# Inverting the 16x16 diagonal blocks of a gated DeltaNet once per group on 128 partitions

## The chip, the cores and the metric

One core of one Trainium2 chip runs the whole program in one launch. The metric is the device time in microseconds (us) from start to end; lower is better. The kernel before is given by three runs, and by one profiled execution from which all rows below come.

## What is computed

Two layers of a model: layer 0 is a bidirectional chunked gated DeltaNet, layer 1 a differential attention. Both work on 512 tokens (256 context, 256 latent) of width 2048. The change touches layer 0 alone, and in it the inverse `tinv` of a unit lower triangular matrix per chunk, head and direction:

```python
lower = jnp.where(strict, jnp.einsum('nbhid,nbhjd->nbhij', kb, kc) * decay, 0.0)
tinv = lax.linalg.triangular_solve(eye + lower, eye, left_side=True, lower=True, unit_diagonal=True)
u = tinv @ (vc * bc[..., None])
w = tinv @ (kb * jnp.exp(gc)[..., None])

def step(s, inp):
    q_i, k_i, u_i, w_i, a_i, gl_i = inp
    v_new = u_i - w_i @ s
    o_i = q_i @ s + a_i @ v_new
    s = s * gl_i[..., None, None] + jnp.einsum('bhck,bhcv->bhkv', k_i, v_new)
```

There are 16 key heads with two value heads each, two directions, and the kernel uses chunks of 128 tokens, so 4 chunks: 2 directions x 4 chunks x 2 value heads = 16 matrices of 128x128 for each key head.

## The kernel before

A **group** g is one key head with its two value heads; there are 16 (g0 to g15). Its four chunks form two **halves** of two. The DeltaNet stage is written as generators (`stream_...`, `filler`), which a small driver (`Drive`) interleaves by priority, by estimated costs and by counted resources (for example `m`: 4, so that the matrices of two groups can be in work). The scheduler of the framework then orders each engine's instructions again by a timeline of its own; every engine runs its list strictly in order.

- `filler` (priority 9, the lowest) makes the projections. One projection tile is 48 matmuls of 128x512 into `pj`; a group has six: q, k, v0, v1, z0, z1. Their weights come in by DMA on SP's queue and are split into two parts by ScalarE (L205, hi) and GpSimd (L207, lo).
- `stream_m` (L741) makes, per half, the matrices I + lower: the products k k^T in `gq`, the decay `grm` (L704, L706), the scaling to `ma` (L712), GpSimd adds the identity (L762), and ScalarE casts to `m16` (L764). `m16` holds eight 128x128 matrices of one half.
- `block_inv` (L715), called once per half, inverts the 16x16 blocks on the diagonal, eight per matrix, 64 blocks in a half. The half is written to HBM (`mb_d`, L718) and its diagonal blocks are read back with one block on each of 64 partitions (`bk`, L720, in pieces of 16 numbers). Then VectorE solves row by row on 64 partitions: two operations make X, the negated block (L725, L726); then for each row i from 1 to 15 one product `bP` (L729) and one sum `bY` (L731). I call these 32 operations a **chain**; each one needs the one before. ScalarE casts the result (L734, L735), and two DMAs put it on the diagonals of two zeroed buffers in HBM (`tu_d`, L737). The tiles of a chain have one buffer each, so chains follow one another.
- `stream_lev` (L770, one for each chunk of a half) loads the block diagonal inverses as `T` and `U` (L791) and merges blocks in three levels (16 to 32, 64, 128): matmuls into `iv`, a masked product `R` on VectorE (L800), casts on ScalarE. The result is `uf`.
- `stream_b` (priority 1) carries the state through the chunks, four steps per group, with matmuls into `sb` and `so` and VectorE operations between them (`y` L891, `yb` L922, `x` L928, `S` L938, `O` L949).
- `stream_at` makes the attention within chunks; `stream_ada` works off modulation rows for later on GpSimd and ScalarE (`rp`, L150, L151).

The wait that ties `stream_m` to the levels before it stands at L748: the matrices of group g, half h, are made only when both chunks' T and U of group g-1, half h, have been loaded, since `mb_d` and `tu_d` have two copies, one per half:

```python
                if g > 0:
                    for p in range(2):
                        yield ev("ld", g - 1, half, p)
```

## Time and profile before

| | us |
|---|---|
| median of 3 runs | 3188.47 |
| fastest and slowest run | 3186.46, 3197.45 |
| span of the profiled execution, first to last instruction | 3172.3 |
| what lies around that span, up to the median run | 16.2 |

The profile gives the span of its execution and no other time of it. Engines are PE (TensorE, matmuls), PEld (its weight loads), DVE (VectorE), ACT (ScalarE), POOL (GpSimd) and SP (the queue that issues nearly all DMAs). A row of groups gives line, engine, operation, written and read tiles, shapes, count, then total busy us and mean ns of one, then the engine's idle time just before it and what ended that. PEclk is the granted share of TensorE's full clock. A busy TensorE is not TensorE at its peak, since matmuls overlap in its pipeline.

### The profile page before, as it was taken

What the parts mean: (1) busy time and instruction counts of PE and PEld (TensorE: products, weight loads), DVE (VectorE), ACT (ScalarE), POOL (GpSimd) and SP (SyncE); (2) the same over time, 40 slices, a digit from 0 to 9 for tenths busy, and PEclk for the clock granted to TensorE, in tenths of its full rate; (3) what the DMA queues carried; (4) which work ended last, traced back from release to release, by engine and by line L of the source; (5) the groups of instructions that cost most, each with busy time, mean ns of one, the idle gap of its engine ahead of it and who ended that gap; (6) DMA issues with size and microseconds to landing.
All of it is one profiled execution on the core that took longest, in us unless ns stands there. A gap on an engine that the chain in (4) does not pass through costs nothing. (4 is left out here: it accounts for less than half of the span.)

```text
span 3172.3 us, 52230 instructions
## 1 busy us (share of the span) xinstructions
PE 2850.3 (90%) x15822; PEld 2251.3 (71%) x15822; DVE 2098.0 (66%) x4728; ACT 1860.8 (59%) x5447; POOL 2052.4 (65%) x2370
## 2 busy tenths in 40 slices
PE   7777898998988898988989988899898999999998
PEld 3455676676776676766767766677686888888888
DVE  7977767769669778678678679632334654544454
ACT  4255675666766666666766756655456665534353
POOL 5876686777777677777767767466466676622334
PEclk8798999998999999999989989999999999999999
DMA  9634445445545555445445445656744555433345
GB/s 336 236 101 115 125 132 123 127 127 131 133 125 134 122 131 134 127 121 136 128 118 142 125 116 131 178 169 192 230 146 129 152 160 161 142 111 110 115 127 163
DMA packets 507185, 457.03 MB, mean 144 GB/s; under 512 B 241171, under 2 KB 383251, under 8 KB 502803
## 3 DMA queue, kind: packets, MB, share of 16 engines
q1 hardware_dynamic: 506900, 453.68, 51.5%
q8 instruction: 124, 2.03, 0.3%
q14 instruction: 159, 1.30, 0.2%
q10 hardware_dynamic: 2, 0.02, 0.0%
HBM read 427.18 MB, written 26.36 MB: 143 GB/s over the span
## 5 line engine op out<-in xcount | busy, mean ns | idle before, releaser
L151 ACT ACTIVATE rp<-rp 128x256 f32<-128x256 f32 x1024 | 426.5, 417 | 344.7 <-POOL rp L150 341.4
L729 DVE TENSOR_TENSOR bP<-bX,bY 64x1 f32<-64x1 f32 (+14 forms) x480 | 225.6, 470 | 15.0 <-ACT bY L727 6.9
L704 DVE SCALAR_TENSOR_TENSOR gra<-gra,gct,cs 128x128 f32<-128x128 f32 x256 | 108.6, 465 | 132.9 <-DMA gra<-gc_d 132.3
L151 ACT ACTIVATION_READ_ACCUMULATOR rp<-rp 128x1 f32 x1024 | 193.8, 189 | 0.0
L704 DVE SCALAR_TENSOR_TENSOR grm<-grm,gct,cs 128x128 f32<-128x128 f32 x256 | 142.7, 602 | 66.3 <-DMA grm<-gc_d 65.6
L800 DVE TENSOR_TENSOR R<-iv,lv 128x512 f16<-128x512 f32 x192 | 126.0, 679 | 29.2 <-PE iv L88 28.8
L167 DVE CUSTOM_DVE_ANT_0 aj<-ar,crow 128x1024 bf16<-128x1024 f32 x80 | 116.3, 1454 | 11.2 <-DMA ar<-in_adaw_dram 9.9
L706 ACT ACTIVATE grm<-grm 128x512 f32<-128x512 f32 x64 | 40.3, 630 | 135.3 <-DVE grm L704 135.3
L762 POOL TENSOR_TENSOR ma<-ma,cs 128x512 f32<-128x512 f32 x64 | 84.8, 1325 | 48.4 <-DVE ma L712 34.7
L731 DVE TENSOR_REDUCE bY<-bP 64x1 f32<-64x1 f32 (+14 forms) x480 | 108.7, 227 | 8.8
L88 PE MATMUL iv<-U,R 128*128 128x128 f16 x768 | 77.2, 225 | 38.3 <-DVE R L800 33.0
L88 PEld LDWEIGHTS <-m 128*128 128x128 f16 x1024 | 73.4, 100 | 51.8 <-issue 46.5
L88 PEld LDWEIGHTS <-R 128*128 128x128 f16 x768 | 47.8, 101 | 83.7 <-DVE R L800 45.7
L706 ACT ACTIVATE gra<-gra 128x512 f32<-128x512 f32 x64 | 40.4, 631 | 106.6 <-DVE gra L704 106.4
L88 PE MATMUL sb<-x,kx 128*128 128x128 f32 x384 | 59.3, 300 | 28.1 <-DVE x L928 28.1
L712 DVE SCALAR_TENSOR_TENSOR at<-gra,beta,gq 128x128 f32<-128x128 f32 x256 | 72.3, 335 | 17.8 <-PE so L88 17.6
L765 POOL TENSOR_TENSOR ml<-ma,m 128x512 bf16<-128x512 f32 x64 | 77.3, 1208 | 6.5 <-ACT m L764 3.2
L817 ACT CAST T<-iv 128x512 f16<-128x512 f32 x128 | 73.4, 574 | 10.4 <-PE iv L88 10.3
L88 PE MATMUL iv<-T,m 128*128 128x128 f16 x768 | 70.8, 223 | 9.5 <-DMA T<-tu_d 4.1
L88 PEld LDWEIGHTS sb<-x,kx 128*128 128x128 f32 x384 | 53.4, 208 | 36.0 <-DVE x L928 33.9
L88 PE MATMUL sb<-yb,uf 128*128 128x128 bf16 x512 | 54.2, 225 | 26.5 <-DVE yb L922 20.4
L88 PE MATMUL so<-x,at 128*128 128x128 f32 x512 | 77.2, 294 | 0.3 <-DVE x L928 0.3
(2763 smaller groups left out, 11506.7 us busy)
## 6 DMA issues: line engine op xcount, KB each, us to landing
aw<-in_adaw_dram SPq DMA_DIRECT2D x512, 128.0 KB, 3.0
ar<-in_adaw_dram SPq DMA_DIRECT2D x32, 1024.0 KB, 6.3
gra<-gc_d SPq DMA_DIRECT2D x128, 128.0 KB, 4.2
grm<-gc_d SPq DMA_DIRECT2D x128, 128.0 KB, 4.2
mb_d<-m SPq DMA_DIRECT2D x32, 256.0 KB, 4.3
U<-tu_d SPq DMA_DIRECT2D x128, 64.0 KB, 2.7
T<-tu_d SPq DMA_DIRECT2D x128, 64.0 KB, 2.5
yd<-sz SPq DMA_DIRECT2D x32, 256.0 KB, 2.9
```

What stands on the lines that cost most here:

```text
L88: nc.tensor.matmul(o, l, r, start=start, stop=stop)
L151: nc.scalar.activation(pr, pr, AF.Copy, accum_out=acc[:, s, q:q + 1])
L167: nc.vector.tensor_tensor_reduce(jk, rq, cr, 1.0, 0.0, ALU.mult, ALU.add, a)
L704: nc.vector.scalar_tensor_tensor(gr[:, u], gr[:, u], gct[:, c, dd, 2 * g + h:2 * g + h + 1], gam[:, s, dd], ALU.subtract, ALU.min)
L706: nc.scalar.activation(gr, gr, AF.Exp)
L712: nc.vector.scalar_tensor_tensor(o[:, u], gr[:, u], beta[:, c, dd, 2 * g + h:2 * g + h + 1], pg, ALU.mult, ALU.mult)
L729: nc.vector.tensor_tensor(pr[:, :i, :i], X[:, i, :i].unsqueeze(1).to_broadcast([64, i, i]), Y[:, :i, :i].rearrange("p j c -> p c j"), ALU. ...
L731: nc.vector.tensor_reduce(Y[:, i, :i], pr[:, :i, :i], AX.X, ALU.add)
L762: nc.gpsimd.tensor_tensor(ma, ma, ident.unsqueeze(1).to_broadcast([P, 4, P]), ALU.add)
L765: nc.gpsimd.tensor_tensor(ml[:, :, k], mv, m16[:, :, k], ALU.subtract)
L800: nc.vector.tensor_tensor(R, quad(pp), lvb(n), ALU.mult)
L817: nc.scalar.copy(Tm, quad(pt))
```

## The change

`block_inv` runs once per group, when both halves' matrices are there, on 128 partitions: 2 directions x 4 chunks x 2 heads x 8 blocks. The buffers `mb_d` and `tu_d` hold 16 matrices in place of 8, and their two copies alternate by group. Each half is written to `mb_d` in two DMAs, one per direction. Both halves' levels wait for the one inversion. `stream_m` waits for the loads of T and U of group g-2, all four chunks, before the first half. The zeroing of `tu_d` takes eight DMAs in place of four.

```diff
@@ -246,8 +246,8 @@
     yd = dram.tile([HV, P, T], F32, name="yd")
     xs_d = dram.tile([KT, P, T], F32, name="xs_d")
     sc_d = dram.tile([2, D], F32, name="sc_d")
-    mb_d = [dram.tile([8, US], F16, name=f"mb_d{i}") for i in range(2)]
-    tu_d = [[dram.tile([8, US], F16, name=f"tu_d{i}{j}") for j in range(2)] for i in range(2)]
+    mb_d = [dram.tile([16, US], F16, name=f"mb_d{i}") for i in range(2)]
+    tu_d = [[dram.tile([16, US], F16, name=f"tu_d{i}{j}") for j in range(2)] for i in range(2)]
     gc_d = dram.tile([NCH, NU, P], F32, name="gc_d")
 
     hp = pool("hp", reuse_waits="tile")
@@ -381,10 +381,11 @@
     zt = dl.tile([P, 1024], F16, name="zt", tag="m16", bufs=4)
     nc.vector.memset(zt, 0.0)
     full = lambda a: a.rearrange("u (j i) -> j u i", i=P)[:P]
-    diag = lambda a: bass.AP(tensor=a[:].tensor, offset=a[:].offset, ap=[[16 * P + 16, 64], [P, 16], [1, 16]])
+    diag = lambda a: bass.AP(tensor=a[:].tensor, offset=a[:].offset, ap=[[16 * P + 16, P], [P, 16], [1, 16]])
     for i in range(2):
         for j in range(2):
-            nc.sync.dma_start(full(tu_d[i][j]), zt.rearrange("p (u i) -> p u i", u=8))
+            for k in range(2):
+                nc.sync.dma_start(full(tu_d[i][j])[:, 8 * k:8 * k + 8], zt.rearrange("p (u i) -> p u i", u=8))
 
     convw = load_small("convw", [P, 4 * KT, 5], d["convw"], dl)
     adt = load_small("adt", [P, 2, 2, HV], d["adt"].to_broadcast([P, NB]).rearrange("p (k d h) -> p k d h", k=2, d=2), dl)
@@ -712,41 +713,40 @@
             nc.vector.scalar_tensor_tensor(o[:, u], gr[:, u], beta[:, c, dd, 2 * g + h:2 * g + h + 1], pg,
                                            ALU.mult, ALU.mult)
 
-    def block_inv(g, half, m16):
-        par = half
-        nm = f"{g}{half}"
-        nc.sync.dma_start(full(mb_d[par]), m16.rearrange("p d c h i -> p (d c h) i"))
-        bk = dl.tile([64, 16, 16], F16, tag="bk", name=f"bk{nm}", bufs=1)
+    def block_inv(g):
+        par = g % 2
+        bk = dl.tile([P, 16, 16], F16, tag="bk", name=f"bk{g}", bufs=1)
         nc.sync.dma_start(bk, diag(mb_d[par]))
-        X = dl.tile([64, 16, 16], F32, tag="bX", name=f"bX{nm}", bufs=1)
-        Y = dl.tile([64, 16, 16], F32, tag="bY", name=f"bY{nm}", bufs=1)
-        pr = dl.tile([64, 16, 16], F32, tag="bP", name=f"bP{nm}", bufs=1)
-        TU = dl.tile([64, 2, 16, 16], F16, tag="bT", name=f"bT{nm}", bufs=1)
-        nc.vector.tensor_scalar(X[:32], bk[:32].rearrange("p j i -> p i j"), -1.0, None, ALU.mult)
-        nc.vector.tensor_scalar(X[32:], bk[32:], -1.0, None, ALU.mult)
-        nc.scalar.copy(Y, e16[:64])
+        X = dl.tile([P, 16, 16], F32, tag="bX", name=f"bX{g}", bufs=1)
+        Y = dl.tile([P, 16, 16], F32, tag="bY", name=f"bY{g}", bufs=1)
+        pr = dl.tile([P, 16, 16], F32, tag="bP", name=f"bP{g}", bufs=1)
+        TU = dl.tile([P, 2, 16, 16], F16, tag="bT", name=f"bT{g}", bufs=1)
+        nc.vector.tensor_scalar(X[:64], bk[:64].rearrange("p j i -> p i j"), -1.0, None, ALU.mult)
+        nc.vector.tensor_scalar(X[64:], bk[64:], -1.0, None, ALU.mult)
+        nc.scalar.copy(Y, e16)
         for i in range(1, 16):
-            nc.vector.tensor_tensor(pr[:, :i, :i], X[:, i, :i].unsqueeze(1).to_broadcast([64, i, i]),
+            nc.vector.tensor_tensor(pr[:, :i, :i], X[:, i, :i].unsqueeze(1).to_broadcast([P, i, i]),
                                     Y[:, :i, :i].rearrange("p j c -> p c j"), ALU.mult)
             nc.vector.tensor_reduce(Y[:, i, :i], pr[:, :i, :i], AX.X, ALU.add)
         for dd in range(2):
-            ps_ = slice(32 * dd, 32 * dd + 32)
+            ps_ = slice(64 * dd, 64 * dd + 64)
             nc.scalar.copy(TU[ps_, dd], Y[ps_])
             nc.scalar.copy(TU[ps_, 1 - dd], Y[ps_].rearrange("p j i -> p i j"))
         for j in range(2):
             nc.sync.dma_start(diag(tu_d[par][j]), TU[:, j])
-        return [tu_d[par][j].rearrange("(d c h) (j i) -> c j d h i", d=2, c=2, i=P) for j in range(2)]
+        return [tu_d[par][j].rearrange("(d c h) (j i) -> c j d h i", d=2, c=4, i=P) for j in range(2)]
 
     def stream_m():
         for g in range(G):
             yield ev("kT", g)
             kT = sts[g]["kT"]
+            if g > 1:
+                for half in range(2):
+                    for p in range(2):
+                        yield ev("ld", g - 2, half, p)
             for half in range(2):
                 yield ("m", 1)
                 yield ("gq", 1)
-                if g > 0:
-                    for p in range(2):
-                        yield ev("ld", g - 1, half, p)
                 nm = f"{g}{half}"
                 m16 = dl.tile([P, 2, 2, 2, P], F16, tag="m16", name=f"m16{nm}", bufs=4)
                 ml = dl.tile([P, 2, 2, 2, P], BF16, tag="ml", name=f"ml{nm}", bufs=4)
@@ -764,8 +764,13 @@
                     nc.scalar.copy(m16[:, :, k], mv)
                     nc.gpsimd.tensor_tensor(ml[:, :, k], mv, m16[:, :, k], ALU.subtract)
                 sts[g].setdefault("m", []).append((m16, ml))
-                sts[g].setdefault("tu", []).append(block_inv(g, half, m16))
-                dr.set("tu", g, half, lat=32)
+                for dd in range(2):
+                    u = 8 * dd + 4 * half
+                    nc.sync.dma_start(full(mb_d[g % 2])[:, u:u + 4], m16[:, dd].rearrange("p c h i -> p (c h) i"))
+                if half == 1:
+                    sts[g]["tu"] = block_inv(g)
+                    for hf in range(2):
+                        dr.set("tu", g, hf, lat=32)
                 free("gq", 1, 14)
                 yield 0.44, 12.0 * LX
 
@@ -779,7 +784,7 @@
                 st = sts[g]
                 c = 2 * half + p
                 m16 = st["m"][half][0]
-                tu = st["tu"][half]
+                tu = st["tu"]
 
                 def t16(tag):
                     return dl.tile([P, 4, P], F16, tag=f"{tag}{p}", name=f"{tag}{g}{c}", bufs=1)
@@ -788,7 +793,7 @@
                 Tm, U = t16("T"), t16("U")
                 for dst, src in ((Tm, tu[0]), (U, tu[1])):
                     for dd in range(2):
-                        nc.sync.dma_start(dst[:, 2 * dd:2 * dd + 2], src[p, :P, dd])
+                        nc.sync.dma_start(dst[:, 2 * dd:2 * dd + 2], src[c, :P, dd])
                 dr.set("ld", g, half, p)
                 yield 0.0, 4.0
                 for n in range(4, 7):

```

The number of chains falls from 32 to 16, and VectorE's list changes where they stand. Inside the first chain of group 4 the list of VectorE had this in the middle (tiles: `grm` decay, `at` attention within the chunk, `S` state, `sz` gate):

```order
L729 TENSOR_TENSOR bP_6891<-bX_6889,bY_6890 64x6x6
L704 SCALAR_TENSOR_TENSOR grm_8098<-grm_8098,gct,cs 128x128 x2
L731 TENSOR_REDUCE bY_6890<-bP_6891 64x6
L704 SCALAR_TENSOR_TENSOR grm_8098<-grm_8098,gct,cs 128x128 x2
L729 TENSOR_TENSOR bP_6891<-bX_6889,bY_6890 64x7x7
L712 SCALAR_TENSOR_TENSOR at_7486<-gra_7478,beta,gq 128x128 x4
L731 TENSOR_REDUCE bY_6890<-bP_6891 64x7
L729 TENSOR_TENSOR bP_6891<-bX_6889,bY_6890 64x8x8
L731 TENSOR_REDUCE bY_6890<-bP_6891 64x8
L938 SCALAR_TENSOR_TENSOR S_6643<-S_6643,egl,sb 128x128
L729 TENSOR_TENSOR bP_6891<-bX_6889,bY_6890 64x9x9
L938 SCALAR_TENSOR_TENSOR S_6643<-S_6643,egl,sb 128x128 x3
```

and in the chain of group 4 it has now:

```order
L728 TENSOR_TENSOR bP_7026<-bX_7024,bY_7025 128x8x8
L730 TENSOR_REDUCE bY_7025<-bP_7026 128x8
L728 TENSOR_TENSOR bP_7026<-bX_7024,bY_7025 128x9x9
L705 SCALAR_TENSOR_TENSOR gra_7869<-gra_7869,gct,cs 128x128
L730 TENSOR_REDUCE bY_7025<-bP_7026 128x9
L705 SCALAR_TENSOR_TENSOR gra_7869<-gra_7869,gct,cs 128x128 x3
L728 TENSOR_TENSOR bP_7026<-bX_7024,bY_7025 128x10x10
L730 TENSOR_REDUCE bY_7025<-bP_7026 128x10
L728 TENSOR_TENSOR bP_7026<-bX_7024,bY_7025 128x11x11
L730 TENSOR_REDUCE bY_7025<-bP_7026 128x11
L728 TENSOR_TENSOR bP_7026<-bX_7024,bY_7025 128x12x12
```

Other work stood between almost any two operations of the chain, 54 instructions in all from its first to its last; now pairs of the chain follow each other, and 32 others stand inside it. Over all chains past the first group there were 11 to 58; now there are 4 to 43, 24 on average.

On SP's queue, the second half of group 6 was written and read back for a chain of its own (tiles: `aw` modulation weights, `gra` and `grm` decay rows, `g7v0r` projection weights):

```order
L718 DMA mb_d_91<-m_10148 128x8x128
L147 DMA aw_0_3_18856<-in_adaw_dram 128x256
L699 DMA gra_10480<-gc_d 128x256 x2
L128 DMA g7v0r_11347<-in_win_dram 128x512
L720 DMA bk_10186<-mb_d_91 64x16x16
```

Now the second write is followed by one read-back for both halves (its first half's write stands 36 rows higher):

```order
L769 DMA mb_d_90<-m_9793 128x4x128 x2
L988 DMA yd<-sz_7622 128x512
L988 DMA yd<-sz_7895 128x512
L147 DMA aw_3_2_17517<-in_adaw_dram 128x256
L128 DMA g6z1r_10785<-in_win_dram 128x512
L719 DMA bk_9832<-mb_d_90 128x16x16
```

The read-back has 128 partitions in place of 64, and the write of a half is two DMAs of four matrices in place of one of eight.

## Rows read from the trace of the kernel before

**Rows 1.** The page's span and busy shares of the whole execution.

```profile
span 3172.3 us, 52230 instructions
...
PE 2850.3 (90%) x15822; PEld 2251.3 (71%) x15822; DVE 2098.0 (66%) x4728; ACT 1860.8 (59%) x5447; POOL 2052.4 (65%) x2370
```

**Rows 2.** TensorE's timeline: start us, us, instruction; first and last of 83 projection tiles.

```profile
374.53 0.50 PE L88 MATMUL pj<-hhi,g2qhi 128*128 128x512 f32 x1 [0.21 <-DVE sz L497]
...
1990.85 0.39 PE L88 MATMUL pj<-hhi,g15z1lo 128*128 128x512 f32 x1
```

**Rows 3.** Busy us of each engine in four bursts and four pauses, in turn.

```profile
core 0: us, PE busy (x) PEld busy (x) DVE busy (x) ACT busy (x) POOL busy (x), PEclk, DMA share, GB/s
469.80:600.40 130.60, 113.31 (x626) 85.62 (x625) 110.02 (x303) 79.27 (x241) 91.47 (x113) 0.93 0.51 125
600.40:702.20 101.80, 94.48 (x579) 73.62 (x578) 60.07 (x137) 70.58 (x228) 75.61 (x102) 0.98 0.49 130
702.20:829.70 127.50, 113.60 (x623) 87.45 (x622) 115.56 (x301) 82.16 (x250) 94.43 (x115) 0.92 0.55 130
829.70:936.20 106.50, 99.34 (x616) 78.34 (x614) 61.86 (x139) 73.38 (x236) 79.04 (x107) 0.97 0.47 129
936.20:1065.80 129.60, 109.91 (x629) 83.17 (x626) 113.60 (x300) 80.71 (x247) 92.26 (x114) 0.97 0.53 130
1065.80:1159.70 93.90, 86.49 (x539) 67.92 (x540) 59.80 (x134) 65.83 (x209) 68.15 (x90) 0.98 0.51 128
1159.70:1289.20 129.50, 114.11 (x654) 87.92 (x652) 117.02 (x309) 83.69 (x254) 94.39 (x117) 0.96 0.52 129
1289.20:1387.10 97.90, 90.07 (x558) 71.16 (x558) 56.63 (x128) 68.90 (x222) 72.68 (x98) 0.97 0.50 130
```

**Rows 4.** TensorE's waits from 400 to 2000 us: total us, times, longest.

```profile
PE iv L88 <- DVE R L800: 28.6, 23, 5.0
PE sb L88 <- DVE x L928: 25.1, 11, 4.0
PE sb L88 <- DVE yb L922: 20.2, 13, 4.0
...
PE iv L88 <- DMA T<-tu_d: 3.8, 5, 2.0
```

**Rows 5.** Groups of the page; then, by shape, from 400 to 2200 us.

```profile
L729 DVE TENSOR_TENSOR bP<-bX,bY 64x1 f32<-64x1 f32 (+14 forms) x480 | 225.6, 470 | 15.0 <-ACT bY L727 6.9
L731 DVE TENSOR_REDUCE bY<-bP 64x1 f32<-64x1 f32 (+14 forms) x480 | 108.7, 227 | 8.8
L712 DVE SCALAR_TENSOR_TENSOR at<-gra,beta,gq 128x128 f32<-128x128 f32 x256 | 72.3, 335 | 17.8 <-PE so L88 17.6
...
L725 DVE TENSOR_SCALAR bX<-bk 32x256 f32<-32x256 f16 x28 | 19.8, 706 | 10.9 <-DMA bk<-mb_d 10.8
L729 DVE TENSOR_TENSOR bP<-bX,bY 64x121 f32<-64x121 f32 x28 | 13.7, 488 | 0.4
```

**Rows 6.** Timelines along the path of group 4's first half.

```profile
675.28 0.66 PE L88 MATMUL gq<-kT 128*128 128x128 f32 x4
...
702.19 0.97 DVE L725 TENSOR_SCALAR bX<-bk 32x256 f32<-32x256 f16 x1 [0.55 <-DMA bk<-mb_d]
...
736.93 0.38 DVE L731 TENSOR_REDUCE bY<-bP 64x15 f32<-64x225 f32 x1
...
742.40 1.95 SPq L791 DMA_DIRECT2D T<-tu_d  x4
...
749.55 0.28 PE L88 MATMUL iv<-T,m 128*128 128x128 f16 x2
```

**Rows 7.** DMA issues: count, KB each, median us from issue to landing.

```profile
T<-tu_d SPq DMA_DIRECT2D x128, 64.0 KB, 2.5
...
tu_d<-bT SPq DMA_DIRECT2D x64, 32.0 KB, 3.1
...
bk<-mb_d SPq DMA_DIRECT2D x32, 32.0 KB, 3.3
```

## Prediction

> **What bounds the kernel now.** I read the page's busy shares first [rows 1]: TensorE is busy 90% of a span of 3172.3 us and VectorE 66%, but these are means over stages with different limits. The diff touches only the DeltaNet stage, so the views that follow are of that stage alone. Its pace is set by the projection tiles (48 matmuls each) that TensorE works through one after another. 83 of them, from g2's q to g15's z1, run from 374.5 to 1991.2 us [rows 2], which is 19.5 us a tile. All other work of TensorE is slotted in between, so whatever stops TensorE inside these 1617 us lengthens the kernel.
>
> The table by stretches [rows 3] is where the reader should look longest. I cut the stage where chains of the 16x16 inversion are running and where they are not. A chain is the two bX operations and 15 pairs bP, bY. The odd rows are bursts (four chains, two groups), the even rows are pauses. Summed over four of each: in bursts (517.2 us) TensorE is busy 87.2%, VectorE 88.2%, granted clock 0.945 on average; in pauses (400.1 us) TensorE 92.6%, VectorE 59.6%, clock 0.975. So TensorE's idle share is 12.8% in a burst and 7.4% in a pause. The list of TensorE's waits says for whom [rows 4]: the three longest are for VectorE, 73.9 us together, and none is for VectorE's chains themselves; they are for R, x and yb, short operations that stand in VectorE's queue among the chains. A wait for T, which is what the chains make, comes to 3.8 us.
>
> **The change part by part.** *VectorE's chains.* Per chain, from the rows of its operations [rows 5]: bP 225.6/32 = 7.05 us, bY 108.7/32 = 3.40 us, the two bX about 0.71 each = 1.42 us; 11.87 us in all. The new chain has the same instructions with the same free sizes on 128 partitions instead of 64. What the partitions cost lies between nothing and double. The nearest rows: a bP of 64x121 takes 488 ns, at of 128x128 takes 335 ns with another operation; twice the partitions at nearly the same length are not dearer, so I take the price of an instruction as unchanged. (If it doubled, VectorE's load would stay as it is: the lower end below.) So 16 of 32 chains go: 190 us of VectorE's 2098. A burst loses two, 23.7 us.
>
> What of that reaches the end? A mean burst is 129.3 us with 114.0 us of VectorE and 112.7 us of TensorE. *Lower end:* TensorE stays idle 12.8%, gain nothing. *Upper end:* the burst becomes a pause in both respects: 112.7 x 0.945/0.975 = 109.2 us of TensorE at 92.6% busy, 118.0 us long, gain 11.3 us a burst, 91 us over eight (16 groups, two a burst). *Taken:* a straight line between the two by VectorE's load. 114.0 - 23.7 = 90.3 us of VectorE in a burst of 123 us is 73%, a bit under half way from 59.6% to 88.2%. The line gives 10.0% idle at clock 0.961: 112.7 x 0.945/0.961 = 110.8, over 0.900 = 123.1 us. That is 6.2 us a burst, **50 us** over eight.
>
> *The wait that is added.* Levels of a group's first half used to wait for that half's chain alone; now for the second half's decay and products too. Who is late next? The path of group 4's first half [rows 6] shows it: products at 675.3, chain from 702.2 to 737.3 (35 us), T issued from 742.4, first level matmul at 749.6. Counted in its new order, TensorE has on average 3.1 projection tiles (2.6 to 3.3 past the first two groups) between the last product of a group and its first level matmul, 60 us at 19.5 us a tile; before it was 3.3 at the head of a burst and 5 to 6 for the other three halves, which had to queue for the single set of chain buffers. What the path needs: from the products to bX 26.9 us, from the chain's end to T landed some 8 us, and a chain that is shorter, since the order of VectorE now has 24 other instructions inside a chain on average, against some 52 at the head of a burst. With 35.1 - 11.9 = 23 us for the 52, 24 cost 11 us, and the chain 23 us. Need 58 us, have 60 us: just in time, as heads of bursts were before. They paid 3.8 us in 5 waits [rows 4], 0.76 us each; now each of 16 groups is a head: 12 us, **8 us more**.
>
> *DMAs.* The write to mb_d becomes two per half (128 KB each), 64 in place of 32; read-backs go from 32 to 16, writes of tu_d from 64 to 32, each twice as large; four zero fills are added. SP issues 12 fewer. Nothing, since they are spread over 2 ms, except landing time. The bk and tu_d transfers in 32-byte pieces land in 3.3 and 3.1 us [rows 7], T, twice the bytes in 256-byte pieces, in 2.5: 1024 pieces against 256 cost 0.8 us at most, so 1024 pieces more should cost about 1.1 us. With twice the pieces the two hops together take between 6.4 us (as now) and 12.8 us (double); I take 8.6 by that slope, which uses up the 2 us above and no more, and keep 12.8 for the third rival. The Trainium skill, DMA: Bandwidth & Descriptors, "Why small descriptors are slow (HBM only)", speaks against this change: each packet carries a fixed overhead, so doubling 32-byte pieces should nearly double the transfer. The trace agrees in direction (2.5 against 3.1 us); by that rule the two hops would take up to 12.8 us, and a chain's result would come 6.4 us later.
>
> *The rest.* ScalarE's copies around a chain halve; ScalarE is busy 63% in bursts [rows 3], no listed long wait is for them, so nothing. m of group g waits for T loads of g-2 in place of g-1: that relaxes a wait. The start: group 0's levels wait for its second half, and TensorE's order has 1.3 more tiles (25 us) ahead of them than before: between nothing and 25 us; nothing, since those tiles are work that has to be done anyhow.
>
> **Sum:** -50 + 8 = -42 us. The profiled execution's span becomes 3130; the median run, 3188.5 us, lies 16.2 us above this span, and I carry those over: 3146 us.
>
> **The rivals.** *1, VectorE is the only bound.* If bursts keep VectorE at 88.2%, they shrink to 90.3/0.882 = 102.4 us, 27 us each, 215 us in all: 2973 us. Against it: 109 us of TensorE would have to fit in. The Trainium skill, Perfetto Trace Analysis, "Identifying the Most-Contended Engine", supports it: it says matmul busy time is no measure of how near TensorE is to its limit, and to optimise the engine with the highest occupancy. This trace bears it out only in part: VectorE leads by one point, and in pauses TensorE leads by 33. 3%. *2, no change.* R, x and yb are links of a dependent sequence (matmul, VectorE, matmul). If TensorE waits for them because of that sequence and not because of VectorE's queue, the waits stay, and GpSimd, busy 72% of a burst, paces the weights as before; the gain stays within 9.6 us: 3188 us. 12%. *3, slower: T comes late.* Place: the first level matmul of each group. TensorE works in order, so all projections behind it wait in full. If both 32-byte hops double, 6.4 us x 16 groups = 102 us, less 50: 3240 us. It decides once T lands later than 60 us after a group's last product; from 3 us per group on it costs more than the change saves. For it: my sum has nothing to spare. Against it: the chains of groups 1, 3 and 5 have fewer than 16 other instructions inside, and a wait lets VectorE catch up. 8%.
>
> **How the numbers follow.** A measurement of this kernel tells 0.3% (9.6 us) from no change. The forecast's case, a gain of more than that, up to 91 us, has 77%. With rival 1, faster is 0.80; same 0.12; slower 0.08. The range 3100 to 3183 runs from nearly the upper end (-88) to a gain of 5 us; it leaves out rivals 1 and 3, half of rival 2 and the tail.
>
> **What would show it.** Right: 240 bP in place of 480, each within a few per cent of 470 ns; VectorE about 1910 us busy; waits for R, x and yb well under 73.9 us; the projections from g2q to g15z1 in about 1575 us. Wrong: a bP on 128 partitions much dearer; waits of iv on T of tens of us (rival 3); waits for R, x and yb unchanged though VectorE is lighter (rival 2).

## The result and the profile after

The changed kernel takes 3213.0 us (median of 4 runs, 3207.6 to 3219.6) against 3189.8 us for the kernel before on the same chip (4 runs, 3186.5 to 3197.5). The ratio is 1.0078 with a 95% interval of 1.0061 to 1.0095: slower by 0.8%, where 1.3% faster was forecast. The time lies above the range.

The page of the changed kernel gives span and busy shares; then come the first and the last projection tile in TensorE's timeline (start us, us, instruction), which answer to [rows 1, 2]:

```profile
span 3207.1 us, 51596 instructions
...
PE 2853.2 (89%) x15822; PEld 2254.9 (70%) x15822; DVE 1914.8 (60%) x4216; ACT 1826.6 (57%) x5367; POOL 2025.1 (63%) x2370
```

```profile
375.32 0.50 PE L88 MATMUL pj<-hhi,g2qhi 128*128 128x512 f32 x1 [0.22 <-DVE sz L498]
...
2029.28 0.40 PE L88 MATMUL pj<-hhi,g15z1lo 128*128 128x512 f32 x1
```

VectorE lost 183 us of work, and the 83 tiles took 1654 us in place of 1617. The 38 us lost in this stage are the whole difference of the two spans (35 us): the stage begins at the same time, and what follows it takes as long as before. Some 12 of these us come with the executions that were profiled and not with the change, since the medians differ by 23 us and the span of before, 3172.3 us, lies some 12 us under that of the fastest run beside the change (a run is about 2 us longer than its span: 3209.3 against 3207.1 us).

The view by stretches, cut at the first and the last tile, shows the stage before (first row) and after (second row). The columns are those of [rows 3]:

```profile
374.53:1991.24 1616.71, 1447.96 (x8459) 1123.77 (x8460) 1225.86 (x3060) 1062.99 (x3307) 1174.93 (x1495) 0.96 0.51 128
```

```profile
375.32:2029.68 1654.36, 1458.31 (x8518) 1128.78 (x8519) 1075.84 (x2627) 1045.83 (x3294) 1169.16 (x1520) 0.95 0.51 127
```

VectorE has 150 us less to do in the stage. TensorE is idle for 1654.36 - 1458.31 = 196.0 us, where it was 168.7: 27 us more. The other 10 us are busy time, at a granted clock of 0.95 in place of 0.96 (means over stretches at 2.4 and at 1.2 GHz).

TensorE's waits from 400 to 2040 us after the change (total us, times, longest), to be read against [rows 4]:

```profile
PE iv L88 <- DVE R L805: 33.8, 28, 5.5
PE sb L88 <- ACT yb L901: 19.9, 15, 4.7
PE iv L88 <- DMA T<-tu_d: 19.6, 17, 3.0
PE sb L88 <- DVE x L933: 17.3, 11, 3.7
PE sb L88 <- DVE yb L927: 11.3, 14, 1.9
```

The waits for R, x and yb on VectorE, which the lighter VectorE was to shorten, went from 73.9 to 62.4 us, and the one for R grew. T went from 3.8 to 19.6 us. ScalarE's yb, too short for the rows of before (4.7 us there), took 19.9 us. VectorE's three lines gave back 11.5 us, and T and ScalarE's yb took 31.

Where did VectorE's time go? These are VectorE's own waits, of the kernel before (400 to 2000 us) and after (400 to 2040 us):

```profile
DVE gra L704 <- DMA gra<-gc_d: 106.5, 66, 7.1
DVE grm L704 <- DMA grm<-gc_d: 56.3, 38, 4.1
DVE R L800 <- PE iv L88: 26.7, 20, 3.6
```

```profile
DVE gra L705 <- DMA gra<-gc_d: 165.2, 77, 8.7
DVE grm L705 <- DMA grm<-gc_d: 121.4, 63, 4.0
DVE R L805 <- PE iv L88: 40.1, 23, 6.0
```

Of the 150 us that are gone from VectorE's stage, 137 us are back as waits on these three lines, nearly all of them for the decay rows that the next product needs. VectorE does its work sooner and then stands.

### The profile page after: what moved, and what is told of

Its sections match the earlier page's. It is cut to its first block, busy times and chain, and to the rows that moved or that the text cites. A ratio compares the mean times of both kernels' runs of the same rounds, so it can differ in the third digit from the quotient of the medians.

```text
span 3207.1 us, 51596 instructions
## 1 busy us (share of the span) xinstructions
PE 2853.2 (89%) x15822; PEld 2254.9 (70%) x15822; DVE 1914.8 (60%) x4216; ACT 1826.6 (57%) x5367; POOL 2025.1 (63%) x2370
## 4 chain that ended last, share of the span: by engine, by line
PE 27%; DMA 9%; DVE 9%; POOL 4%; ACT 4%; issue 3%; SPq 1%; DVEq 0%; POOLq 0%; ACTq 0%
PE pj L88 24%; POOL rp L150 2%; DMA grm<-gc_d 2%; DMA gra<-gc_d 2%; DMA aw<-in_adaw_dram 2%; PE at L88 1%; DVE grm L705 1%; DVE bP L728 1%; ACT rp L151 1%; DMA xs_d<-xb 1%; DVE gra L705 1%; PE iv L88 0%; DMA yr<-yd 0%; PE sb L88 0%; DMA tu_d<-bT 0%
## 5 line engine op out<-in xcount | busy, mean ns | idle before, releaser
L705 DVE SCALAR_TENSOR_TENSOR gra<-gra,gct,cs 128x128 f32<-128x128 f32 x256 | 96.7, 417 | 187.0 <-DMA gra<-gc_d 186.1
L728 DVE TENSOR_TENSOR bP<-bX,bY 128x1 f32<-128x1 f32 (+14 forms) x240 | 113.3, 472 | 5.2
L88 PEld LDWEIGHTS <-uf 128*128 128x128 f16 x512 | 36.2, 100 | 60.3 <-issue 51.4
L713 DVE SCALAR_TENSOR_TENSOR ma<-grm,beta,gq 128x128 f32<-128x128 f32 x256 | 72.1, 339 | 8.1 <-ACT grm L707 3.5
L823 ACT CAST U<-iv 128x512 f16<-128x512 f32 x128 | 75.6, 590 | 0.0
```

The lines of the kernel that those rows point to most:

```text
L88: nc.tensor.matmul(o, l, r, start=start, stop=stop)
L705: nc.vector.scalar_tensor_tensor(gr[:, u], gr[:, u], gct[:, c, dd, 2 * g + h:2 * g + h + 1], gam[:, s, dd], ALU.subtract, ALU.min)
L713: nc.vector.scalar_tensor_tensor(o[:, u], gr[:, u], beta[:, c, dd, 2 * g + h:2 * g + h + 1], pg, ALU.mult, ALU.mult)
L728: nc.vector.tensor_tensor(pr[:, :i, :i], X[:, i, :i].unsqueeze(1).to_broadcast([P, i, i]), Y[:, :i, :i].rearrange("p j c -> p c j"), ALU.mult)
L823: nc.scalar.copy(U, quad(pu))
```

## The experiments

Ratios are to the kernel before, run on the same chip beside them. There it took 3182.2 us for e1 to e4, 3182.4 for e5 to e8, 3180.5 for e9 to e12, 3179.6 for e13 to e16 and 3183.7 for e17 and e18, so rows are compared by their ratios. "Fused" is the changed kernel, "halves" the kernel before. Path is worked out from the traces: from a group's last product `gq` to its first level matmul, mean of the fused kernels' groups 2 to 14. For halves it is the mean of the first halves of these 13 groups; the second halves, which queue behind them, take longer (101.5 us in the kernel before).

| run | us | ratio, 95% interval | VectorE busy us | path us |
|---|---|---|---|---|
| the kernel before | 3189.8 | 1 | 2098.0 | 90.0 |
| the change | 3213.0 | 1.0078 (1.0061 to 1.0095) | 1914.8 | 63.5 |
| e1 fused, chain cut | 3110.5 | 0.9774 (0.9746 to 0.9802) | 1798.7 | 42.7 |
| e2 halves, chain cut | 3103.9 | 0.9750 (0.9729 to 0.9771) | 1807.9 | 47.4 |
| e3 fused, decay rows doubled | 3184.3 | 1.0012 (0.9999 to 1.0025) | 1932.4 | 62.6 |
| e4 halves, relaxed load wait | 3181.9 | 0.9996 (0.9982 to 1.0009) | 2083.2 | 87.7 |
| e5 fused, one more hop | 3209.2 | 1.0079 (1.0064 to 1.0094) | 1925.8 | 64.6 |
| e6 fused, load put back | 3186.1 | 1.0012 (1.0002 to 1.0021) | 2082.4 | 60.4 |
| e7 fused, k first | 3163.6 | 0.9935 (0.9920 to 0.9950) | | 60.0 |
| e8 fused, smaller pools | 3178.4 | 0.9990 (0.9977 to 1.0002) | | 61.2 |
| e9 halves, smaller pools | 3182.2 | 1.0007 (0.9993 to 1.0021) | | 87.2 |
| e10 halves, k first | 3218.5 | 1.0114 (1.0092 to 1.0136) | | 63.6 |
| e11 halves, added load | 3257.8 | 1.0241 (1.0220 to 1.0261) | 2363.3 | 96.4 |
| e12 fused, e7 and e8 | 3181.9 | 1.0000 (0.9988 to 1.0012) | | 62.7 |
| e13 fused, planner 36 | 3171.5 | 0.9977 (0.9963 to 0.9992) | 1927.2 | 65.2 |
| e14 halves, planner 36 | 3145.2 | 0.9896 (0.9872 to 0.9920) | 2098.0 | 87.2 |
| e15 fused, planner 26 | 3174.6 | 0.9987 (0.9974 to 0.9999) | | 67.3 |
| e16 halves, planner 26 | 3158.9 | 0.9942 (0.9918 to 0.9966) | | 84.8 |
| e17 fused, chain and load tripled | 3514.0 | 1.1043 (1.1011 to 1.1076) | 2653.1 | 146.8 |
| e18 halves, load behind both chains | 3229.7 | 1.0140 (1.0107 to 1.0173) | 2364.9 | 96.9 |

**Does the chain itself matter (e1, e2).** Both kernels with the chain cut after its first row:

```diff
-        for i in range(1, 16):
+        for i in range(1, 2):
```

> The changed kernel with the chain cut to its first pair of operations: rows 2 to 15 of every 16x16 block are left out, so a chain is 2 pairs shorter by 14 of 15 and takes some 3 us in place of the 24 us its trace shows. Theory L (late chain: every group's levels now wait for one chain that starts only when the second half is there, and TensorE, in order, waits for T): the 19.6 us of waits for T and what follows from them go, 3212.98 us falls to 3150 or lower and is no longer above the equally cut kernel before (within 0.3%). Theory D (VectorE's lighter queue arrives at the decay operations before their rows have landed, and stands there): VectorE is lighter still, its waits for gra and grm stay at 280 us or grow, the time stays at 3195 or above, some 20 us above the cut kernel before. Theory S (only the scheduler's new order and the relaxed wait for the loads cost, not the fused chain): some 20 us above the cut kernel before.

> The kernel before with the same cut: rows 2 to 15 of every block left out, 32 chains of one pair. It is the measure for the fused kernel with the cut. VectorE loses 14/15 of 334 us. Theory L: half of the groups had a late chain too, so this gains, to some 3140 to 3165 us. Theory D: no gain or a few us, 3180 to 3200. Theory S: as D.

Both became faster, by 2.3% and 2.5%, and they end together, 0.9774 and 0.9750. This is one order of each kernel; further down, orders of one kernel differ by 1%, so that what else the change does (the later start of a first half's inverse, the wider transfers, the relaxed wait) shows no cost beyond that. The gain does not go by the work taken off: 290 us off the halves and 116 us off the fused kernel lead to the same time (and to the same load, some 1800 us).

Theory L had the sign of both runs, D and S did not. But L's cause is not there. TensorE's waits for T in e1, from 375 to 2030 us, are not gone; they are longer than the 19.6 us of the change, though the path is 21 us shorter:

```profile
PE iv L88 <- DMA T<-tu_d: 26.2, 16, 4.0
```

And in e2 the waits for x, R and yb are 69.5 us where the kernel before has 75.6 in the same window, with 290 us less work on VectorE:

```profile
PE sb L88 <- DVE x L928: 25.7, 10, 5.3
PE iv L88 <- DVE R L800: 24.7, 21, 2.8
PE sb L88 <- DVE yb L922: 19.1, 12, 3.8
```

Part of the gain lies outside the stage of the 83 tiles: of the difference of the spans, 31 of 96 us in e1 and 42 of 68 us in e2. What makes a kernel with a cut chain faster stays open.

**The parts one by one (e3 to e6).** e3 gives the decay rows `grm` and `gra` two buffers each (with `qT` at 2 and `uf` at 6 to make room); e4 gives the halves the relaxed wait alone; e5 sends the diagonal blocks of each group once more to HBM and back; e6 puts 15 pairs of VectorE work, which nobody reads, behind each fused chain.

```diff
# e3 (the line that matters; its smaller pools are those of e8 below)
-        gr = dl.tile([P, 4, P], F32, tag=tag, name=f"{tag}{g}{c}", bufs=1)
+        gr = dl.tile([P, 4, P], F32, tag=tag, name=f"{tag}{g}{c}", bufs=2)
# e4 (left out: four copies of mb_d and tu_d in place of two)
-        par = half
+        par = 2 * (g % 2) + half
-                if g > 0:
+                if g > 1:
-                        yield ev("ld", g - 1, half, p)
+                        yield ev("ld", g - 2, half, p)
# e5 (left out: the new tiles bk0 and hop_d)
-        nc.sync.dma_start(bk, diag(mb_d[par]))
+        nc.sync.dma_start(bk0.rearrange("p (j i) -> p j i", j=16), diag(mb_d[par]))
+        nc.sync.dma_start(hop_d[par], bk0)
+        nc.sync.dma_start(bk, hop_d[par].rearrange("p (j i) -> p j i", j=16))
# e6
+        for i in range(1, 16):
+            nc.vector.tensor_tensor(pr[:, :i, :i], X[:, i, :i].unsqueeze(1).to_broadcast([P, i, i]),
+                                    X[:, :i, :i].rearrange("p j c -> p c j"), ALU.mult)
+            nc.vector.tensor_reduce(X[:, 0, :i], pr[:, :i, :i], AX.X, ALU.add)
```

> The changed kernel with two buffers in place of one for each of the decay tiles grm and gra; to make room, qT has 2 buffers in place of 3 and uf 6 in place of 8. Theory D: the loads are issued a product earlier, VectorE's waits for gra and grm fall from 287 us to under 100, and the time falls to 3190 us or lower. Theory L: those waits fall too, but the waits of TensorE for T stay near 20 us and the time stays within 0.5% of 3213 us. Theory S: the order moves again, by up to 10 us either way.

> The kernel before with one part of the change alone: four copies of mb_d and tu_d (by group parity and half), so that the matrices of a half wait for the loads of group g-2 in place of g-1, with the 32 chains on 64 partitions kept. Theory L and theory D: within 0.3% of 3190 us, since the chains and VectorE's load are those of before. Theory S: 3205 us or more.

> The changed kernel with latency added to each chain and no work on VectorE: the diagonal blocks read back go once more to HBM and back before the chain starts (two more DMAs of 64 KB in series per group, some 4 us each, 8 to 9 us per group). Theory H (what counts is the time from a group's last product to its first levels, summed over the groups that wait for it: 31 us of the end per 100 us of chain, from the two cut kernels): 16 x 8.5 = 136 us more, so some 35 to 50 us slower than the changed kernel. Theory V (VectorE's load and order count, not the chain's length): within 10 us of the changed kernel.

> The changed kernel with VectorE's load given back and the chain's result not delayed: behind each chain, after its result is cast, 15 more pairs of the same shapes run on tiles that nobody reads (170 us of VectorE over the stage, 1914.8 to some 2080 us busy). Theory H: no later T, so within 15 us of the changed kernel. Theory V: VectorE's saved time is spent again, 30 us slower or more.

e4: the relaxed wait shows no cost (0.9996). e5: the hop shows none against the change, as theory V had it, but the DMA view of e5 with the path shows that this says nothing for V. The issues (KB each, median us from issue to landing) are:

```profile
bk<-mb_d SPq DMA_DIRECT2D x16, 64.0 KB, 3.8
...
hop_d<-bk SPq DMA_DIRECT2D x16, 64.0 KB, 4.3
bk<-hop_d SPq DMA_DIRECT2D x16, 64.0 KB, 1.9
```

From the matrices to bX it takes 15.8 us in place of 10.0, as the two transfers say. But the chain behind it takes 19.5 us in place of 24.0, because some 19 other VectorE instructions run inside it on average where the change has some 27, and the path ends only 1.1 us longer. So e5 did not test a late T; it showed that the order is made anew around an edit.

e6 tests VectorE's load. Its page has VectorE at 2082 us, within 1% of the kernel before:

```profile
PE 2841.9 (89%) x15822; PEld 2250.9 (71%) x15822; DVE 2082.4 (65%) x4696; ACT 1825.0 (57%) x5367; POOL 2031.5 (64%) x2370
```

168 us of work came back, for which the prediction's line asks 46 us, 1.4%. By the ratios the kernel came out 0.7% faster than the change, which neither theory had, and 0.2% above the mean of the six fused kernels below. e3 was faster too, by 0.7%, but not by what it was meant to do: VectorE's waits for decay rows fell by a tenth only (gra 144, grm 117 us from 375 to 2030, against 172 and 121). That two unrelated edits each gave 0.7% back made me suspect the order in which the instructions happen to be written.

**Is it the order (e7 to e10, e12).** e7 projects the k tile of the group after next ahead of the next group's v tiles; e8 is e3 without its point, the smaller pools alone. e9 and e10 are the same two edits on the halves, and e12 has both on the fused kernel.

```diff
# k first (e7, e10, e12)
-            seq += [("z0", g), ("z1", g), ("q", g + 1), ("v0", g + 1), ("v1", g + 1), ("k", g + 2)]
+            seq += [("z0", g), ("z1", g), ("q", g + 1), ("k", g + 2), ("v0", g + 1), ("v1", g + 1)]
# smaller pools (e8, e9, e12): the driver's counts (left out: the tiles' bufs, 2 and 6 with them)
-    res = {k: Res(n) for k, n in dict(pj=2, th=2, kT=3, qT=3, v=3, sz0=2,
-                                      sz1=2, gq=1, m=4, uf=8, at=3).items()}
+    res = {k: Res(n) for k, n in dict(pj=2, th=2, kT=3, qT=2, v=3, sz0=2,
+                                      sz1=2, gq=1, m=4, uf=6, at=3).items()}
```

> The changed kernel with the k projection of group g+2 made before the v projections of g+1 (one line of the filler's sequence), so that the keys from which a group's products are made are there two projection tiles (some 38 us) earlier. Theory H: the path to T starts earlier against the state steps that need it; the time falls by 25 us or more, to 3185 or lower. Theory V: the order of the projections is nothing to VectorE's load; within 10 us of the changed kernel.

> The control of the kernel with two decay buffers: the changed kernel with qT at 2 buffers and uf at 6, the decay tiles at one as before. If the second decay buffer gave that kernel its gain of some 28 us, this one stays within 8 us of the changed kernel; if the smaller pools moved the order and gave it, this one is near 3184 us too.

> The kernel before with two buffers for qT in place of three and six for uf in place of eight, the edit that took the fused kernel from 3213 to 3178 us (e8_fused_slim). The work and its dependencies are the same; what moves is the order that the scheduler writes down. Theory O (the 0.8% of the change is mostly the particular order that the scheduler happened to write; fusing by itself is worth about nothing, since several fused kernels lie between 3178 and 3213): this kernel lies anywhere in 3170 to 3205, and near the fused one with the same edit, ratio of e8 to it 0.995 to 1.005. Theory T (fusing costs by itself, since the inverses of a first half wait for the blocks of all four chunks; the fused kernel gained 1.1% by the edit because the edit helps either kernel): 3145 to 3160, so that fused over halves is again 1.006 to 1.010.

> The kernel before with the one edit of e7_fused_kfirst: the k tile of the group after next is projected ahead of the two v tiles of the next group, so that a group's m-work has its input two tiles (about 39 us) earlier. That edit took the fused kernel from 3213 to 3164 us. Theory O: 3150 to 3180, and e7 over this is 0.995 to 1.005. Theory T: the halves keep their lead, 3130 to 3145, e7 over it 1.006 to 1.010. A third reading (the fused chain needs its input early and the halves do not): no gain here, 3180 to 3200.

> The changed kernel with both edits that made it faster by themselves, the smaller pools of e8 (3178 us) and the earlier k of e7 (3164 us). If each gains by what it does to the waits of the stage, they add: 3125 to 3145. If both only trade one order of the scheduler for another (theory O), they do not: 3150 to 3190.

By the ratios, smaller pools took 0.9% (28 us) off the fused kernel, nothing off the halves; so e3 needed no second buffer for its gain. k first took 1.4% (45 us) off the fused kernel, as theory H of e7 had it, and *added* 1.1% (38 us) to the halves, which none of the three readings of e10 had, and the two gains of the fused kernel do not add: together (1.0000) they give no more than the smaller one alone. Theory O was right on e9 and e12; for e7 over e10 it had allowed 0.995 to 1.005, and 0.982 is farther apart than it said. Its cause, the earlier path, does not carry over to e10: there the path became 26 us shorter (63.6 for 90.0 us) and the kernel slower. After these edits the fused kernel is ahead of the halves by 0.2% and by 1.8%, where the change as it stands is behind by 0.8%.

**The order alone (e13 to e16).** The driver assumes 32 us from the inverse's instructions to the first level. Another number changes no operation, buffer or dependency, only the order in which instructions are written:

```diff
# fused; the halves have the same number at their line
-                        dr.set("tu", g, hf, lat=32)
+                        dr.set("tu", g, hf, lat=36)
```

> The changed kernel with 36 in place of 32 for the latency that the planner assumes from the inverse's instructions to the first level (a number that only sets the order in which instructions are written; operations, buffers and dependencies are the same). Theory O (most of the 0.8% is the particular order): the fused times scatter over 3170 to 3215 whatever this number is, and this one differs from the 3213 of the change by anything up to 40 us, more likely below it than above (3175 to 3205). Theory T (the fused chain costs by itself): 3200 to 3225, and about 25 us above the halves with the same number.

> The kernel before with 36 in place of 32 for the same latency. Theory O: the halves scatter as the fused ones do, 3165 to 3220, and e13 over this is as likely under 1 as over. Theory T: 3170 to 3195, about 25 us under e13.

> The changed kernel with 26 for the same latency. Theory O: 3170 to 3215. Theory T: 3200 to 3225, about 25 us above the halves with 26. If it is the lateness of T that the planner has wrong (TensorE waits 19.6 us for T's loads in the changed kernel), a smaller number brings the levels ahead, makes these waits longer and the time worse than 3213, and 36 makes them shorter.

> The kernel before with 26 for the same latency. Theory O: 3165 to 3220, on either side of e15. Theory T: 3170 to 3195, about 25 us under e15.

All four are faster than with 32, on both sides of it, the fused kernel by 1.0% and 0.9% against the change, the halves by 1.0% and 0.6%. There is no trend in the number, neither for the time nor for T: TensorE's waits for T in the fused kernel, from 375 to 2030 us, are 8.3 us with 36 and 7.4 us with 26, where 32 has 19.6; the smaller number was expected to make them longer. Theory O had the fused kernels right. The halves went lower than it said (3145 and 3159). Theory T had the fused ones wrong (3200 to 3225) and the distance between the two about right in one pair (26 us with 36, 16 us with 26).

The stage of e13 (first row) and of e14 (second row), cut as the two rows of the stage above:

```profile
374.20:1989.98 1615.78, 1439.64 (x8427) 1123.66 (x8428) 1073.42 (x2598) 1038.43 (x3234) 1156.16 (x1501) 0.96 0.51 129
```

```profile
374.76:1968.84 1594.08, 1430.27 (x8459) 1102.31 (x8460) 1221.36 (x3059) 1068.41 (x3315) 1175.47 (x1499) 0.98 0.51 130
```

TensorE is idle 176.1 us in e13 and 163.8 us in e14. e13 has VectorE as light as the change and needs 39 us less for the same tiles, 20 us of it idle and 19 us busy time. e14 has VectorE as loaded as the kernel before and is the fastest of all kernels with the whole computation, 1.0% under the kernel before and 1.8% under the change (0.9896 over 1.0078). In its stage only 5 us of the gain are idle time; 18 us are busy time, with as many matmul records (8459), at a granted clock of 0.98 in place of 0.96. It is the version to keep.

**The same change in five variants.** Fused over halves: 1.0078 as it stands, 0.9983 with smaller pools, 0.9823 with k first, 1.0082 with 36, 1.0045 with 26; mean 1.0002, standard deviation 0.011. Taken singly, the six fused kernels of this kind (the change, e7, e8, e12, e13, e15) have a mean ratio of 0.9995 and the five halves (before, e9, e10, e14, e16) 0.9992, with standard deviations of 0.5% and 0.8%. So a 0.8% difference between one fused and one halves kernel is no more than two orders of one kernel differ by, though each ratio is measured to 0.2%. What fusing is worth by itself is 0.0% with an uncertainty of about 1% (two standard errors of the difference of the two means, 0.4% each). This zero needs all five variants, and two of them change more than the order: smaller pools change buffers and k first the sequence of the projections. In the three pairs that differ in the planner's number alone the fused kernel is the slower one each time (1.0078, 1.0082, 1.0045; mean 0.7%). Three pairs do not set that apart from chance, since one number moves either kernel by up to 1.0%, but a cost of the fused chain by itself, as theory T has it, is not excluded.

**More load (e11, e17, e18).** e11 puts the 15 unread pairs of e6 behind every half's chain; e18 puts 30 pairs behind the second half's chain and none between the two. e17 was to put 45 pairs behind the fused chain.

```diff
# e11 on the halves: the four lines of e6 with 64 partitions; e18 has for its loop
+        for i in 2 * half * list(range(1, 16)):
# e17, as it ran: the loop of e6 and that of the chain itself
-        for i in range(1, 16):
+        for i in 3 * list(range(1, 16)):
```

> The kernel before with 15 more pairs of a multiplication and a reduction behind each half's chain, on numbers that nobody reads: VectorE's busy time goes up by about 340 us (32 chains of 11 us), most of it inside the DeltaNet stage. The step that the prediction rested on (a straight line from VectorE's load to TensorE's idle share: 50 us for 183) would make it some 85 to 95 us slower, 3270 to 3280. Theory L (VectorE's load in this range has next to no effect, as e6_fused_load said where 130 us more cost nothing): 3170 to 3215. In between, 3215 to 3260: the load counts, but above a threshold that the kernel before does not reach.

> The changed kernel with 45 dummy pairs behind each group's chain (three times e6_fused_load's 15): some 390 to 540 us more VectorE time than in the changed kernel, in all more than e11_halves_load has. Theory W (load counts only above what the kernel before has: TensorE's waits for VectorE grow when VectorE's queue has less slack than a group needs): 3240 to 3290. Theory P (e11's loss is the place: its dummy work stands ahead of the second half's chain and puts that off by 11 us): 3170 to 3215, as the other fused kernels. The straight line of the prediction, 50 us for 183, would make it 105 to 145 us above the fused kernels' mean of about 3188: 3290 to 3330.

> The kernel before with the whole dummy load of e11_halves_load (30 pairs a group) behind the second half's chain, none between the two chains of a group. Theory W: as e11, 3235 to 3275. Theory P: 3165 to 3220, as the unloaded halves (3145 to 3218 in the runs so far).

e17 is not the kernel of its expectation. The edit hit the chain's own loop too, so the chain runs its 15 pairs three times in the path, as its page shows (L728 is the chain, L738 the load):

```profile
L728 DVE TENSOR_TENSOR bP<-bX,bY 128x1 f32<-128x1 f32 (+4 forms) x720 | 346.5, 481 | 14.8
L738 DVE TENSOR_TENSOR bP<-bX 128x1 f32<-128x1 f32 (+4 forms) x720 | 320.2, 445 | 15.3
```

It decides nothing between the theories W and P. It does give one more point for the path: 146.8 us long, 83 more than in the change, for a time some 330 us above the fused kernels' mean (1.1043 against 0.9995); e1's path is 21 us shorter and its time 70 us less. That is 4.0 and 3.4 us for each us of path in 16 groups. But the two points differ in VectorE's load as well. And two things speak against the path as the cause: e10, slower with a path 26 us shorter, and the unloaded fused kernels, which with paths of 60 to 67 us are on average no faster than the halves with 85 to 90 (e10 apart).

e11 and e18 added 265 and 267 us of VectorE (busy 2363 and 2365 us, fewer than the 340 I had put down) and cost 77 and 46 us. e11 lies in the middle one of its three ranges, the load counting only from some point above that of the kernel before; e18 lies between its two ranges, which decides neither for W nor for P. Both are above every unloaded halves kernel, e18 by little (1.0140 against 1.0114 of e10). So load above that of the kernel before probably does count, 0.17 to 0.29 us for each us, where the prediction's line has 0.27 (50 for 183); with 0.8% between orders of the halves, e18 alone would not show it. Whether e11 lost more because its load stands ahead of the second chain is open: the 31 us between them are within what orders differ by.

## Why the prediction was wrong

- **VectorE's chains: right.** 240 bP at 472 ns (470 forecast from [rows 5]), bY at 235 (227 before), VectorE busy 1914.8 us (about 1910). Twice the partitions cost next to nothing:

```profile
L728 DVE TENSOR_TENSOR bP<-bX,bY 128x1 f32<-128x1 f32 (+14 forms) x240 | 113.3, 472 | 5.2
```

- **DMAs: right.** The two hops in 32-byte pieces take 7.8 us together, where 8.6 was taken and 12.8 kept for the third rival, by the DMA view of the changed kernel against [rows 7]:

```profile
T<-tu_d SPq DMA_DIRECT2D x128, 64.0 KB, 2.5
...
tu_d<-bT SPq DMA_DIRECT2D x32, 64.0 KB, 4.0
...
bk<-mb_d SPq DMA_DIRECT2D x16, 64.0 KB, 3.8
```

  The Trainium skill, DMA: Bandwidth & Descriptors, "Why small descriptors are slow (HBM only)", states a fixed overhead per packet; that the time would nearly double with the pieces is what the prediction took from it. Here twice as many, with twice the bytes, take 1.15 times as long for bk and 1.29 times for tu_d. These medians are not sharp: the same bk transfer has 3.1 us in e6 and 4.6 in e13. e5 shows where the pieces do count: the read back of the same 64 KB takes 1.9 us where each partition's 512 bytes lie together and 3.8 us in 32-byte pieces, while the write is no cheaper in whole pieces (4.3 us) than in small ones (4.0).

- **The wait for T: right in kind, mis-sized.** The term was 8 us more than the 3.8 of before (0.76 us in each of 16 groups). It came to 19.6 us in 17 waits, 1.15 each: 15.8 us more. The path of group 4's first half took 64 us where the forecast needs 58 and has 60 (63.5 on average): TensorE's product, VectorE's first and last operation of the chain, SP's issue of T and the first level, to be read against [rows 6]:

```profile
690.79 0.66 PE L88 MATMUL gq<-kT 128*128 128x128 f32 x4
...
719.10 0.38 DVE L724 TENSOR_SCALAR bX<-bk 64x256 f32<-64x256 f16 x1 [0.42 <-DMA bk<-mb_d]
...
743.47 0.39 DVE L730 TENSOR_REDUCE bY<-bP 128x15 f32<-128x225 f32 x1
...
750.24 1.97 SPq L796 DMA_DIRECT2D T<-tu_d  x4
...
755.11 0.29 PE L88 MATMUL iv<-T,m 128*128 128x128 f16 x2
```

  So the path was sized 6 us too short, and a path with no slack is waited for. How much depends on the order: 7.4 and 8.3 us in e15 and e13, 24.6 in e8, which is nevertheless faster than the change.

- **The step that failed: 50 us by a straight line from VectorE's load to TensorE's idle share.** The line was drawn through bursts (88.2% VectorE, 12.8% idle) and pauses (59.6%, 7.4%) [rows 3], as if the load made the idle time. With 150 us less load in the stage TensorE's idle time did not fall by it; it went from 168.7 to 196.0 us. The stretches of the changed kernel, the chains of groups 4 to 9 and the pauses behind them in turn, show that the line of before does not hold in it:

```profile
core 0: us, PE busy (x) PEld busy (x) DVE busy (x) ACT busy (x) POOL busy (x), PEclk, DMA share, GB/s
719.10:743.90 24.80, 20.94 (x92) 14.90 (x92) 20.86 (x65) 14.99 (x54) 17.20 (x23) 0.93 0.40 126
743.90:833.30 89.40, 76.74 (x451) 60.31 (x450) 50.23 (x108) 55.14 (x165) 64.42 (x84) 0.94 0.53 129
833.30:850.10 16.80, 16.02 (x102) 12.55 (x101) 16.02 (x48) 10.63 (x40) 13.53 (x19) 1.00 0.42 130
850.10:938.80 88.70, 80.06 (x460) 62.39 (x459) 61.13 (x140) 57.83 (x179) 64.15 (x84) 0.92 0.56 134
938.80:958.40 19.60, 16.53 (x110) 12.44 (x109) 16.05 (x47) 12.34 (x45) 12.65 (x16) 1.00 0.35 106
958.40:1073.00 114.60, 101.74 (x595) 80.78 (x594) 68.97 (x164) 73.71 (x231) 80.64 (x107) 0.93 0.50 124
1073.00:1096.40 23.40, 17.16 (x83) 11.96 (x82) 20.05 (x60) 13.71 (x48) 14.13 (x18) 0.97 0.46 110
1096.40:1179.00 82.60, 73.57 (x440) 56.68 (x439) 45.98 (x103) 51.14 (x152) 59.75 (x79) 0.97 0.57 131
1179.00:1200.80 21.80, 17.88 (x104) 14.12 (x103) 17.86 (x48) 12.10 (x44) 14.68 (x19) 0.92 0.50 116
1200.80:1295.40 94.60, 81.40 (x487) 64.51 (x486) 56.99 (x143) 57.95 (x175) 61.46 (x81) 0.91 0.52 124
1295.40:1316.70 21.30, 19.17 (x105) 14.35 (x104) 20.59 (x56) 14.02 (x52) 17.57 (x23) 1.00 0.38 114
1316.70:1424.80 108.10, 97.10 (x580) 75.53 (x579) 66.87 (x154) 69.54 (x214) 74.58 (x100) 0.95 0.50 128
```

  In the six pauses (578.0 us) VectorE is busy 350.2 us, 61%, about what it was in the pauses of before; TensorE is busy 510.6 us and so idle 11.7%, not 7.4%. In the six stretches with a chain, which became short (127.7 us, 21 us a group), VectorE is busy 87% and TensorE idle 15.7%. So the two still go together from stretch to stretch, but the same load of VectorE, that of a pause, now comes with another idle share of TensorE. My reading, which no run tests by itself: the idle time belongs to work that each group has to do anyway, the levels and the state's steps, where matmul, VectorE or ScalarE and matmul take turns (the waits for R, x and yb), and in the kernel before much of that lay beside the chains. Two rows that differ in the load differ in all else that lies there too. e6, with the load put back into the fused kernel, is 0.2% above the fused kernels' mean, where the line asks 1.4% and their spread is 0.5%. Only above the load of the kernel before did more load cost time (e11, and by little e18).

- **The rivals.** The second, no change, had the mechanism nearest to what the runs show: waits for R, x and yb that belong to a dependent sequence and stay when VectorE gets lighter (62.4 of 73.9 us are left, and ScalarE's yb alone took more than the difference; in e2, with 290 us off VectorE, 69.5 of 75.6). They are not untouched, though: in e1, with 116 us off, 43.4 of the change's 62.2 us are left from 375 to 2030 us. Over six fused kernels the mean is that rival's time, 0.9995. The third had the right sign for this one run by luck: the hops did not double, and T's waits do not go with the time (e8 and e1 have longer ones and are faster). The first, 2973 us, was far off. It stood on the Trainium skill, Perfetto Trace Analysis, "Identifying the Most-Contended Engine", which says to work on the engine with the highest occupancy, and to judge TensorE by MFU and weight loads and not by its busy matmuls. In bursts VectorE was that engine (88.2%, with 66.5% for the weight loads [rows 3]), but 183 us off it gave nothing.

- **The 16.2 us around the span: mis-sized, without effect.** A run is about 2 us longer than its span (3209.3 and 3207.1 us in the profiled run of the change); the rest of the 16.2 is that the profiled execution of before was shorter than the median run. The forecast is 42 us under that median either way.

- **What the forecast did not have.** The 0.8% itself. No rival said that rewriting the order moves the time by about 1% either way, whatever the change is meant to do. The forecast took 0.3% as what a measurement tells from no change; that holds for one kernel measured again, not for two kernels whose orders differ.

Open stay the effect of fusing by itself inside 1% (nothing, or the 0.7% of the three pairs), why a shortened chain pays, and whether a place in the order costs the change its 0.8%, and which. An order in which the changed kernel keeps every instruction where the kernel before has it was not tried.

## What to carry to other kernels

Where a scheduler writes the order, one build of a change is one draw: move numbers that set nothing but the order, for the kernel before and for the changed one, more often than the three times here, before a difference of 1% is put down to the change, and keep the best draw (here 1.0% for a single number). And ask of a busy engine whether it stands elsewhere in the same stage: VectorE waited 163 us for decay rows there, and 287 us when 150 us of work had been taken off it in the stage; a slope read across two kinds of stretches tells where things lie, not what they cause.

## What the runs showed of the hardware that was not expected

In e5 a 64 KB read from HBM took half as long in 512-byte pieces as in 32-byte pieces (1.9 against 3.8 us), while a write of 64 KB did not gain (4.3 us in 512-byte pieces, 4.0 in 32-byte pieces in the change). The two writes stand at different places of the program, and no run has them alone.

The order by itself moved the granted clock, and with it the busy time: in the stage of e14 as many matmul records (8459) were busy 18 us less than in the kernel before, at 0.98 in place of 0.96. Over whole runs e14 has 0.962 to 0.966, the kernel before beside it 0.954 to 0.962.
